# One layer with an RWKV-7 and a GLA mixer on one core: both heads of a pair multiplied by VectorE in one order, and chunk inverses from blocks of 16 joined by TensorE

## The chip, the cores and the metric

One core of one Trainium2 chip runs the whole kernel. The metric is device time in microseconds of one execution, the median of several runs. All arithmetic is fp32; wide matmuls are done as three products of rounded high and low halves.

## The reference, cut to what matters

An encoder layer works on two sequences of 512 and 256 tokens (768 together), model width 1024: a mixer, cross attention and a feed-forward net, each with norms. The mixer has eight RWKV-7 heads of width 64 and four GLA heads. An RWKV head keeps a 64x64 state S per direction (forward and backward) and goes from token to token:

```python
sa = einsum('bhij,bhj->bhi', S, -kk_t)
S = S * w_t[:, :, None, :] + sa[..., None] * (kk_t * a_t)[:, :, None, :] + v_t[..., None] * k_t[:, :, None, :]
y = einsum('bhij,bhj->bhi', S, r_t)
```

The kernel does this in chunks of 64 tokens, twelve in all. Within a chunk the products of decayed `kk` and `kk*a` make a strictly triangular 64x64 matrix N, and the chunk needs the inverse of I - N. That inverse is what half of this change is about.

## The kernel before, in words

Heads go in pairs p = 0 to 3, one head on partitions 0 to 63 and one on 64 to 127. For each pair, and each direction d:

- `prep` (L692) loads the projections, makes running sums of the decays, and with them two pair tiles: `bk_of` (L660) multiplies `kk*a` and `k` by the inverse decays, `ar_of` (L669) `kk` and `r` by the decays. Each of the eight products of a direction's two tiles covers one head (64 partitions, 12 chunks of 64): the first head's on VectorE (`dve`), the second's on GpSimd (`pool`). In the second head the two halves of a tile lie the other way round, so that a later matmul finds them in the order in which it wants them. `to_places` writes the tiles to DRAM (`bkd`, `ard`).
- `lower` (L678) makes N by 64x64 matmuls, copies it to `lsb`, and writes its 32x32 diagonal blocks to DRAM (`ld`).
- `inverses` (L731) reads the blocks of both directions so that each block lies in one partition (48 blocks a direction, 112 partitions with a gap), and inverts them there: 31 steps of a product and an addition on VectorE (L744, L746) on up to 256 elements a partition, in the tiles `snf`, `sqf`, `stmp`. Plain (`qd`) and transposed (`td`) results go to DRAM.
- `join` (L772) loads them back with channels on partitions (`tt`, `tdz`) and makes the missing 32x32 corner of each 64x64 inverse by two rounds of 32x32 matmuls, merge1 (L788) and merge2 (L800), 24 a direction; then the matrix goes to DRAM (`ttd`).
- `products` (L973) loads a group of four chunks of a pair and makes the matrices of a recurrence step; it transposes `bkg` for both heads (L1000).
- `stage(q)` (L1134) runs four `step`s (L1007) for up to three jobs: the recurrence, a chain that goes TensorE, ScalarE, TensorE, ScalarE, TensorE, VectorE and on to the next step.

Around them run other matmuls: the dense projections of the mixer (L247), the GLA heads (`gla_head`, L825), and sixteen `memory_block`s (L1104) for the cross attention's keys and values. The program is written pair by pair (`begin`, `invert`, `joined`), but the order on each engine is set by a scheduler from priorities: `high_priority(offset=...)` of 2000 for `begin` and `invert`, 6000 for `joined`, 4000 for the steps, 3000 for `products`. Each engine then works through its queue in that order. All transfers are issued by SyncE through `dma` (L41). In PSUM there are few banks: `psn` has one buffer, `psm` two.

## Time and profile before

| | |
|---|---|
| median of 3 runs | 1593.78 us (1593.54 to 1599.62) |
| profiled execution | 1596.87 us, span 1595.0 us |
| TensorE matmul busy | 1442.8 us, 90% of the span |
| VectorE, ScalarE, GpSimd busy | 1049.7, 718.9, 514.6 us |
| mean granted TensorE clock | 0.914 |
| DMA packets under 512 B | 89264 of 279565 |

The mixer's parts lie from about 120 to 840 us: `prep` of pairs 0 to 3 from about 142, 310, 467 and 542 us, the recurrence's steps from 444 to 826 us. After that come the output projection, the cross attention and the feed-forward net. A line of a view names the line of the kernel, the engine, the operation, and output<-inputs; x384 for 192 matmuls in the program means that the trace has two instructions for an fp32 matmul.

### The profile page before, as it was taken

To read this page: it belongs to the slowest core of one execution; us is meant where nothing else is said; L and a number is where in the kernel's file an instruction comes from. 1 tells how busy PE (TensorE), PEld (TensorE's weight loads), DVE (VectorE), ACT (ScalarE), POOL (GpSimd) and SP (SyncE) were. 2 spreads that over 40 slices of the span, in tenths; PEclk is the share of its full clock that TensorE was granted. 3 is DMA by queue.
4 is the path that set the end of the run, shared out by engine and by line. 5 is a ranking of instruction groups with operands and counts; after the bars stand their busy time and mean duration, and the time that the engine had idled before them with its cause. 6 is when DMAs were issued, how large, how long until landed. Compare 5 with 4: busy or idle time off the path is not lost. (4 is left out here: it accounts for less than half of the span.)

```text
span 1595.0 us, 28271 instructions
## 1 busy us (share of the span) xinstructions
PE 1442.8 (90%) x10614; PEld 1246.0 (78%) x10614; DVE 1049.7 (66%) x1605; ACT 718.9 (45%) x1417; POOL 514.6 (32%) x576
## 2 busy tenths in 40 slices
PE   7999689889887889899888999996999999999996
PEld 6887578777775777778767888786999999787785
DVE  5545885497577795764455434448876676878886
ACT  5754344443333332333344354434555556544442
POOL 6416643494317342211531354420000001231223
PEclk9999798989875988888979999997999999999998
DMA  6686555556468447754452333235555447564434
GB/s 168 181 302 188 167 137 131 145 146 192 111 205 229 127 149 176 205 134 135 126 166 99 119 95 105 73 111 160 172 169 176 158 145 284 171 204 132 143 100 142
DMA packets 279565, 250.35 MB, mean 157 GB/s; under 512 B 89264, under 2 KB 227059, under 8 KB 279428
## 3 DMA queue, kind: packets, MB, share of 16 engines
q1 hardware_dynamic: 279428, 248.54, 52.1%
q8 instruction: 84, 1.38, 0.4%
q14 instruction: 53, 0.43, 0.1%
HBM read 164.11 MB, written 82.58 MB: 155 GB/s over the span
## 5 line engine op out<-in xcount | busy, mean ns | idle before, releaser
L148 POOL TENSOR_TENSOR wlo<-wraw,whi 128x256 fp32r<-128x256 f32 x192 | 176.8, 934 | 331.0 <-ACT whi L147 231.1
L247 PE MATMUL pd<-hT_hi,whi 128*128 128x256 f32 (+1 forms) x512 | 182.0, 356 | 12.6 <-DVE gd L325 8.2
L247 PE MATMUL pd<-hT_hi,wlo 128*128 128x512 f32 (+1 forms) x512 | 180.1, 354 | 4.0 <-POOL wlo L148 4.0
L247 PE MATMUL pd<-hT_lo,whi 128*128 128x256 f32 (+1 forms) x512 | 178.6, 350 | 0.3 <-DVE hT_lo L206 0.3
L1511 POOL TENSOR_TENSOR wl<-w,wh 128x1024 fp32r<-128x1024 f32 x8 | 21.2, 2649 | 329.8 <-ACT wh L1510 329.8
L247 PEld LDWEIGHTS pd<-hT_hi,whi 128*128 128x128 f32 x512 | 100.4, 196 | 27.6 <-issue 5.5
L247 PEld LDWEIGHTS pd<-hT_hi,wlo 128*128 128x128 f32 x512 | 99.6, 195 | 18.6 <-POOL wlo L148 5.3
L147 ACT ACTIVATE whi<-wraw 128x256 fp32r<-128x256 f32 x192 | 77.3, 414 | 78.2 <-PE pd L1104 22.9
L247 PEld LDWEIGHTS pd<-hT_lo,whi 128*128 128x128 f32 x512 | 100.4, 196 | 13.0 <-DVE hT_lo L206 0.5
L148 DVE TENSOR_TENSOR ul<-ur,uh 128x768 fp32r<-128x768 f32 x56 | 77.4, 1388 | 30.7 <-ACT uh L147 17.7
L147 ACT ACTIVATE uh<-ur 128x768 fp32r<-128x768 f32 x56 | 47.4, 847 | 107.8 <-PE gz L1520 52.0
L1510 ACT ACTIVATE wh<-w 128x1024 fp32r<-128x1024 f32 x64 | 67.1, 1053 | 35.9 <-PE fz L1520 24.2
L1520 PE MATMUL gx<-wh,uh 128*128 128x512 f32 x192 | 75.0, 397 | 4.3 <-DVE acc L1713 4.3
L1511 DVE TENSOR_TENSOR wl<-w,wh 128x1024 fp32r<-128x1024 f32 x56 | 68.2, 1219 | 15.1 <-ACT wh L1510 14.5
L1520 PE MATMUL gx<-wl,uh 128*128 128x512 f32 x192 | 75.9, 395 | 0.0
L1520 PE MATMUL gx<-wh,ul 128*128 128x512 f32 x192 | 75.4, 395 | 0.0
L1520 PE MATMUL fz<-hh,wh 128*128 128x384 f32 x192 | 66.0, 344 | 1.9 <-ACT wh L1510 1.9
L1511 POOL TENSOR_TENSOR wl<-ws,wh 128x1024 fp32r<-128x1024 f32 x16 | 40.6, 2536 | 79.6 <-ACT wh L1510 79.6
L1520 PE MATMUL fz<-hh,wl 128*128 128x384 f32 x192 | 65.2, 344 | 0.8 <-DVE wl L1511 0.8
L1520 PE MATMUL fz<-hl,wh 128*128 128x384 f32 x192 | 65.8, 343 | 0.0
L1510 ACT ACTIVATE wh<-ws 128x1024 fp32r<-128x1024 f32 x48 | 50.5, 1052 | 26.8 <-PE fx L1520 22.3
L1104 PE MATMUL pd<-mem_hi,whi 128*128 128x256 f32 x256 | 59.3, 308 | 1.4 <-ACT mo L1116 1.4
(476 smaller groups left out, 4306.9 us busy)
## 6 DMA issues: line engine op xcount, KB each, us to landing
w<-in_w_ff_dram SPq DMA_DIRECT2D x64, 512.0 KB
ur<-ud SPq DMA_DIRECT2D x56, 384.0 KB
wraw<-in_w_in_dram SPq DMA_DIRECT2D x108, 128.0 KB
ud<-u SPq DMA_DIRECT2D x32, 384.0 KB
ud<-us SPq DMA_DIRECT2D x24, 384.0 KB
wraw<-in_wkv_x_dram SPq DMA_DIRECT2D x64, 128.0 KB
lora<-lo_t SPq DMA_DIRECT2D x20, 384.0 KB
bkg<-bkd SPq DMA_DIRECT2D x24, 256.0 KB
```

The source lines that it names most:

```text
L147: act.activation(out=hi, in_=src, func=AF.Copy)
L148: (lo_eng or pool).tensor_tensor(out=lo, in0=src, in1=hi, op=ALU.subtract)
L247: pe.matmul(out=out, lhsT=a, rhs=b, start=(i == 0), stop=(i == n - 1))
L1104: prev = order_after(pe.matmul(out=pd[:, c0:c0 + 256], lhsT=x, rhs=y[:, c0:c0 + 256], start=(k + i + c0 == 0), stop=(k + i + c0 == KD + 25 ...
L1510: act.activation(out=hi, in_=t[name], func=AF.Copy)
L1511: lo_eng.tensor_tensor(out=lo, in0=t[name], in1=hi, op=ALU.subtract)
L1520: pe.matmul(out=out, lhsT=a, rhs=b, start=first and i == 0, stop=last and i == n - 1, skip_group_check=True)
```

## The change

Two parts. **The products.** `bk_of` and `ar_of` now write both heads in one order, with one VectorE instruction over 128 partitions in place of one over 64 on VectorE and one over 64 on GpSimd. What read the second head in its old order is changed to match: `lower` and `products` take other indices, the load of `ard` for the second head becomes two transfers, and the transposes of the second head's `bkg` become four transposes of 64x64 and four matmuls by the identity, since the halves must change places.

**The inverses.** `lower` writes blocks of 16x16 (eight transfers in place of four a direction), `inverses` inverts pairs of those in 15 steps on up to 128 elements, and writes plain and transposed results into one tensor. `join` loads them into `inv` (plain and transposed, two 16x16 blocks on a diagonal of a 32x32 block that is zero elsewhere), and the off-diagonal 16x16 blocks of N from `lsb` into `offb`. Then for each direction: merge0 (48 matmuls of 32x32), an addition of the identity on VectorE, merge0t (24) and merge0m (48), and six copies on ScalarE; that gives what was loaded before. merge1 and merge2 follow as they were; merge2's copies go from VectorE to ScalarE. merge0 to merge0m use `psn` for the forward and `psm` for the backward direction, `tdz` now lies in `snf` and `stmp`, and the sums in `sqf` and `sxf`.

Since `snf`, `sqf` and `sxf` have become smaller, two of the planes for the output projection's weights and half of a gain row move to `inv` and `offb`; `t1` has two buffers in place of three.

```diff
     def bk_of(pinv, nka, kd):
         b_ = pair_tile()
-        dve.tensor_tensor(out=b_[0:64, :, 0, :], in0=v3(nka, 0, 64), in1=v3(pinv, 0, 64), op=ALU.mult)
-        pool.tensor_tensor(out=b_[64:128, :, 1, :], in0=v3(nka, 64), in1=v3(pinv, 64), op=ALU.mult)
-        dve.tensor_tensor(out=b_[0:64, :, 1, :], in0=v3(kd, 0, 64), in1=v3(pinv, 0, 64), op=ALU.mult)
-        pool.tensor_tensor(out=b_[64:128, :, 0, :], in0=v3(kd, 64), in1=v3(pinv, 64), op=ALU.mult)
+        dve.tensor_tensor(out=b_[:, :, 0, :], in0=v3(nka), in1=v3(pinv), op=ALU.mult)
+        dve.tensor_tensor(out=b_[:, :, 1, :], in0=v3(kd), in1=v3(pinv), op=ALU.mult)
...
-        for j in range(4):
-            dma(lds[st["p"]][d][:, j], lt[j * 32:(j + 1) * 32, :, (j % 2) * 32:(j % 2) * 32 + 32])
+        for j in range(8):
+            c = j % 4 * 16
+            dma(lds[st["p"]][d][j % 2, :, j // 2], lt[j * 16:(j + 1) * 16, :, c:c + 16])
...
-        for j in range(31):
-            nr, ni = j + 1, 31 - j
-            tm = stmp[:, 0:nr * ni].rearrange("p (a b) -> p a b", a=nr)
...
+        for j in range(15):
+            nr, ni = j + 1, 15 - j
+            tm = stmp[0:112, 0:2 * nr * ni].rearrange("p (e a b) -> p e a b", e=2, a=nr)
+            dve.tensor_tensor(out=tm, in0=sq[:, :, 0:nr, j:j + 1].broadcast_to([112, 2, nr, ni]),
+                              in1=sn[:, :, j:j + 1, j + 1:16].broadcast_to([112, 2, nr, ni]), op=ALU.mult)
+            dve.tensor_tensor(out=sq[:, :, 0:nr, j + 1:16], in0=sq[:, :, 0:nr, j + 1:16], in1=tm, op=ALU.add)
...
+            for j in range(8):
+                e, x = j % 2, j % 2 * 16
+                dma(invs[d][j * 16:j * 16 + 16].rearrange("p c q x -> p (c q) x")[:, :, x:x + 16],
+                    qd[d][e, :, j // 2].rearrange("s c q t -> s (c q) t"))
             for j in range(4):
-                rs = slice(j * 32, j * 32 + 32)
-                dma(tt[d][rs, :, (j % 2) * 32:(j % 2) * 32 + 32], qd[d][:, j])
-                if j % 2 == d:
-                    dma(tdz[d][rs], td[d][:, j])
+                r, c = 32 * j + 16 * d, j % 2 * 32 + 16 * (1 - d)
+                dma(offb[r:r + 16, d, :, 16 * (1 - d):16 * (1 - d) + 16], lts[d][r:r + 16, :, c:c + 16])
+        for d in range(2):
...
+            pm = bank("merge0")
+            for c in range(NCH):
+                for g in G:
+                    pe.matmul(out=pm[g, c, :], lhsT=offb[g, d, c, :], rhs=inv[g, c, 1, :], start=True, stop=True)
+            dve.tensor_tensor(out=fi, in0=pm, in1=bc(i32, NCH), op=ALU.add)
+            pm = bank("merge0t")
+            for c in range(NCH):
+                for g in G[d::2]:
+                    pe.matmul(out=pm[g, c, :], lhsT=inv[g, c, 0, :], rhs=fi[g, c, :], start=True, stop=True)
+            for g in G[d::2]:
+                act.activation(out=tdz[d][g], in_=pm[g], func=AF.Copy)
+            pm = bank("merge0m")
+            for c in range(NCH):
+                for g in G:
+                    pe.matmul(out=pm[g, c, :], lhsT=fi[g, c, :], rhs=inv[g, c, 0, :], start=True, stop=True)
+            for j, g in enumerate(G):
+                act.activation(out=tt[d][g, :, j % 2 * 32:j % 2 * 32 + 32], in_=pm[g], func=AF.Copy)
...
-            for h in (0, 64):
-                dve.tensor_copy(out=tt[d][h + o0:h + o0 + 32, :, o1:o1 + 32], in_=pn[h + o0:h + o0 + 32])
+            for h in (0, 64):
+                act.activation(out=tt[d][h + o0:h + o0 + 32, :, o1:o1 + 32], in_=pn[h + o0:h + o0 + 32], func=AF.Copy)
...
-        for h, hs in enumerate(HS):
-            dma(a_[hs, :, h:h + 2, :].rearrange("p u i x -> p u (i x)"), ard[p][hs, g])
+        dma(a_[HS[0], :, 0:2, :].rearrange("p u i x -> p u (i x)"), ard[p][HS[0], g])
+        for i in range(2):
+            dma(a_[HS[1], :, 2 - i, :], ard[p][HS[1], g, :, i * 64:i * 64 + 64])
...
-                pe.transpose(out=pt[:, u, :], in_=fl(b_[HS[h], u]), identity=ident[HS[h], HS[h]])
+                if h == 0:
+                    pe.transpose(out=pt[:, u, :], in_=fl(b_[HS[0], u]), identity=ident[HS[0], HS[0]])
+                else:
+                    pe.transpose(out=pt[HS[0], u, :], in_=b_[HS[1], u, 1, :], identity=ident[HS[1], HS[1]])
+                    pe.matmul(out=pt[HS[1], u, :], lhsT=b_[HS[1], u, 0, :], rhs=ident[HS[1], HS[1]], start=True, stop=True)
```

The scheduler's order moves with it. On TensorE, at pair 0's join, the order before had merge1 of the two directions (tiles `tdz`) with the last products of a GLA head (L913, L915) between them:

```order
L247 MATMUL pd<-hT_lo,whi 128x512
L788 MATMUL merge_2046<-tdz_1478,lsb 32x32 x24
L913 MATMUL go<-arena 128x64 x2
L915 MATMUL go<-arena 128x128
L913 MATMUL go<-arena 128x64 x2
```

Now the join comes while that GLA head has not begun its matmuls, among dense projections (L247). First the first rounds, with one lone merge0 ahead of them:

```order
L812 MATMUL merge_2028<-inv_1470,offb 32x32
L247 MATMUL pd<-hT_lo,whi 128x512
L247 MATMUL pd<-hT_hi,wlo 128x512
L247 MATMUL pd<-hT_hi,whi 128x512
L247 MATMUL pd<-hT_lo,whi 128x512
L247 MATMUL pd<-hT_hi,wlo 128x512
L247 MATMUL pd<-hT_hi,whi 128x512
L812 MATMUL merge_2028<-inv_1470,offb 32x32 x45
L812 MATMUL merge_2158<-inv_1474,offb 32x32 x37
L817 MATMUL merge0t<-sqf,inv_1470 32x32 x24
L812 MATMUL merge_2158<-inv_1474,offb 32x32 x11
```

Then, some twenty dense matmuls on, the rest in one piece:

```order
L247 MATMUL pd<-hT_hi,whi 128x256
L823 MATMUL merge0m<-inv_1470,sqf 32x32 x48
L817 MATMUL merge0t<-sxf,inv_1474 32x32 x24
L823 MATMUL merge0m<-inv_1474,sxf 32x32 x48
L833 MATMUL merge_2288<-snf,lsb 32x32 x24
L907 MATMUL gs<-arena 64x64 x12
```

The join moves ahead of the GLA head's matmuls, and the merges of the two directions alternate. On VectorE, in pair 0's inversion, the steps before stood among the evacuations of dense products (L322, L325):

```order
L744 TENSOR_TENSOR stmp<-sqf,snf 112x87
L322 SCALAR_TENSOR_TENSOR gd<-pd,cv,gd 128x511
L746 TENSOR_TENSOR sqf<-sqf,stmp 112x3x29
L325 SCALAR_TENSOR_TENSOR gd<-pd,cv,gd 128x511
L744 TENSOR_TENSOR stmp<-sqf,snf 112x112
L746 TENSOR_TENSOR sqf<-sqf,stmp 112x4x28
```

Now the same stretch of the inversion is:

```order
L761 TENSOR_TENSOR stmp<-sqf,snf 112x78
L763 TENSOR_TENSOR sqf<-sqf,stmp 112x2x3x13
L761 TENSOR_TENSOR stmp<-sqf,snf 112x96
L763 TENSOR_TENSOR sqf<-sqf,stmp 112x2x4x12
L761 TENSOR_TENSOR stmp<-sqf,snf 112x110
L763 TENSOR_TENSOR sqf<-sqf,stmp 112x2x5x11
```

Its first nine steps stand one behind the other with nothing between. On TensorE, at the recurrence's last steps, the order before had no memory blocks left, and output projections (`po`) between the steps (`rec`):

```order
L1049 MATMUL rec<-pl_5344 64x64 x4
L247 MATMUL po<-w_snf,mix_bk 128x512 x2
L247 MATMUL po<-w_sqf,mix_bk 128x512
L247 MATMUL po<-w_snf,mix_bk 128x512
L247 MATMUL po<-w_pl_9175,mix_bk 128x512 x3
L247 MATMUL po<-w_sqf,mix_bk 128x512
```

Now memory blocks (L1154 in the changed kernel) stand there:

```order
L1099 MATMUL rec<-pl_5841 64x64 x4
L1154 MATMUL pd<-mem_hi,whi 128x256
L1154 MATMUL pd<-mem_lo,whi 128x256 x2
L1154 MATMUL pd<-mem_hi,wlo 128x256 x2
L1154 MATMUL pd<-mem_hi,whi 128x256 x2
L1154 MATMUL pd<-mem_lo,whi 128x256 x2
```

The joins and the later steps have moved ahead of memory blocks: when the last step is reached, 672 of the 768 memory-block matmuls have been issued in the new order, and all 768 in the old one.

More of the change, by code (lines that the diff above doesn't have):

```diff
@@ L610 @@
         tts.append(t)
-        tdz.append(mp.tile([P, NCH, 32], F32, name=f"tdz{d}"))
+        t = mp.tile([P, NCH, 2, 32], F32, tag=f"inv{d}", name=f"inv{d}")
+        pool.memset(t, 0.0)
+        invs.append(t)
+    offb = mp.tile([P, 2, NCH, 32], F32, tag="offb", name="offb")
+    pool.memset(offb, 0.0)
+    i32 = mp.tile([P, 32], F32, name="i32")
+    for j in range(4):
+        rs = slice(32 * j, 32 * j + 32)
+        pool.tensor_copy(out=i32[rs], in_=ident[rs, rs])
     px = mp.tile([P, NCH, 66], F32, tag="px", name="px")
@@ L615 @@
     px_prev = (px[:, :, 0:64], px[:, :, 2:66])
[L616 to L618 removed]
+    snf, sqf, sxf = (mp.tile([P, 512], F32, tag=n, name=n) for n in ("snf", "sqf", "sxf"))
+    sn, sq, sx = (t[0:112].rearrange("p (e a b) -> p e a b", e=2, a=16) for t in (snf, sqf, sxf))
+    stmp = mp.tile([P, NCH * 32], F32, tag="stmp", name="stmp")
     pool.memset(sn, 0.0)
```

78 lines of the change are left out of this document (40 added, 38 removed).

## Prediction

> **What bounds the kernel now.** First the busy time of each engine by stretch (the columns are named in the head row; every field is a stretch's length, then busy time and instructions of an engine, then the TensorE clock that was granted). Two long stretches hold the mixer; eight short ones the places where VectorE is fullest, and the end of the recurrence.
>
> ```profile
> core 0: us, PE busy (x) PEld busy (x) DVE busy (x) ACT busy (x) POOL busy (x), PEclk, DMA share, GB/s
> 120.00:440.00 320.00, 276.36 (x1969) 232.64 (x1970) 223.35 (x278) 139.75 (x251) 169.74 (x165) 0.87 0.56 152
> 440.00:840.00 400.00, 348.01 (x4387) 291.33 (x4385) 263.90 (x598) 146.64 (x398) 133.71 (x150) 0.83 0.59 164
> ...
> 142.00:204.00 62.00, 47.49 (x328) 39.31 (x328) 50.97 (x36) 24.63 (x43) 46.41 (x41) 0.76 0.54 155
> 208.00:254.00 46.00, 40.14 (x263) 33.48 (x263) 44.08 (x88) 20.72 (x39) 16.31 (x19) 0.96 0.51 137
> 312.00:352.00 40.00, 34.51 (x227) 29.59 (x226) 38.94 (x25) 21.16 (x38) 38.07 (x25) 0.89 0.52 148
> 375.00:427.00 52.00, 45.14 (x235) 39.03 (x235) 41.07 (x79) 18.17 (x33) 15.63 (x13) 0.87 0.48 120
> 472.00:512.00 40.00, 26.47 (x322) 22.40 (x320) 32.99 (x43) 14.29 (x41) 31.87 (x27) 0.50 0.81 220
> 540.00:602.00 62.00, 52.52 (x733) 45.28 (x729) 58.66 (x116) 21.07 (x59) 30.07 (x24) 0.87 0.45 134
> 643.00:695.00 52.00, 45.50 (x612) 39.96 (x610) 47.50 (x129) 20.36 (x57) 10.86 (x15) 0.90 0.59 174
> 792.00:812.00 20.00, 10.02 (x88) 6.94 (x89) 14.36 (x29) 7.18 (x21) 14.22 (x21) 0.54 0.55 168
> ```
>
> TensorE is the engine that everything waits for in the end, and I count its loss as a stretch's length less busy time times granted clock, an estimate from above, since it takes a matmul at half the clock to last twice as long (the bursts quoted below last 0.95 and 1.49 us). From 120 to 440 us that is 320 - 276.36 x 0.87 = 80 us, from 440 to 840 us 400 - 348.01 x 0.83 = 111 us: 191 us in all. The four stretches in which `prep` runs (from 142, 312, 472 and 540) lose 25.9 + 9.3 + 26.8 + 16.3 = 78 us, with VectorE 82 to 97% busy; three in which `inverses` runs (208, 375, 643) lose 7.5 + 12.7 + 11.1 = 31 us at 79 to 96%; the recurrence's last steps (792) lose 14.6 us.
>
> Second, what the two engines do there: the groups by line, with mean ns, and the idle time before each at the end.
>
> ```profile
> L744 DVE TENSOR_TENSOR stmp<-sqf,snf 112x31 f32<-112x31 f32 (+15 forms) x124 | 53.1, 428 | 3.3
> L746 DVE TENSOR_TENSOR sqf<-sqf,stmp 112x31 f32<-112x31 f32 (+15 forms) x124 | 50.4, 406 | 3.0
> L685 PE MATMUL low<-bk 64*64 64x64 f32 x384 | 23.3, 267 | 16.6 <-DVE bk L672 16.6
> L674 POOL TENSOR_TENSOR bk<-r,px 64x768 f32<-64x768 f32 x8 | 19.2, 2396 | 0.0
> L672 DVE TENSOR_TENSOR bk<-kk,px 64x768 f32<-64x768 f32 x8 | 18.6, 2331 | 0.0
> L673 POOL TENSOR_TENSOR bk<-kk,px 64x768 f32<-64x768 f32 x8 | 18.5, 2306 | 0.0
> L663 DVE TENSOR_TENSOR bk<-wb,wa 64x768 f32<-64x768 f32 x8 | 18.1, 2267 | 0.0
> L675 DVE TENSOR_TENSOR bk<-r,px 64x768 f32<-64x768 f32 x8 | 17.2, 2145 | 0.0
> ```
>
> The two lines of the inversion take 103.5 us of VectorE. The products take more than 2.1 us apiece on either engine. Third, the order of time on VectorE shows why, and how long the inversion lasts by the clock: its first copy (L738) and its last (L752) for pairs 2 and 3, then two small steps of it.
>
> ```profile
> 159.23 0.95 DVE L665 TENSOR_TENSOR bk<-kds,wa 64x768 f32<-64x768 f32 x1
> 191.59 0.96 DVE L654 TENSOR_TENSOR wc<-wc,k 128x768 f32<-128x768 f32 x1
> 192.86 2.50 DVE L665 TENSOR_TENSOR bk<-wc,wa 64x768 f32<-64x768 f32 x1
> ...
> 526.84 0.69 DVE L738 COPY snf<-sxf 48x1024 f32<-48x1024 f32 x1 [5.13 <-DMA sxf<-ld]
> 608.71 1.04 DVE L752 COPY snf<-sqf 48x1024 f32<-48x1024 f32 x1
> 643.38 0.69 DVE L738 COPY snf<-sxf 48x1024 f32<-48x1024 f32 x1 [7.33 <-DMA sxf<-ld]
> 693.68 1.59 DVE L752 COPY snf<-sqf 48x1024 f32<-48x1024 f32 x1
> ...
> 208.97 0.19 DVE L744 TENSOR_TENSOR stmp<-sqf,snf 112x31 f32<-112x31 f32 x1
> 214.67 0.30 DVE L744 TENSOR_TENSOR stmp<-sqf,snf 112x135 f32<-112x135 f32 x1
> ```
>
> The same product lasts 0.95 us in one place and 2.50 us in the other, where GpSimd works on its own half beside it; a 128x768 product, twice the partitions, lasts 0.96 us. So the split between two engines gains nothing: each slows the other. And pair 2's inversion takes 83 us by the clock, pair 3's 52 us, because other VectorE work is queued between its steps. These two stand one behind the other: pair 3's cannot start before pair 2's `join` has left `sqf`, and the last two long stages of the recurrence need what they make. TensorE's order of time has the place where stage 2 waits for pair 2's matrix:
>
> ```profile
> 652.02 0.69 PE L1031 MATMUL rec<-rh,pl 64*64 64x64 f32 x8 [4.59 <-DMA pl<-ttd]
> ```
>
> The end of the kernel, from 880 us on, is dense TensorE work that the change does not touch; what the mixer gains or loses, the whole does.
>
> **The products, part by part.** Of 32 products of 64 rows on VectorE and 32 on GpSimd, 32 of 128 rows on VectorE are left. L663, L672 and L675 alone fall from 53.9 us to 24 x 0.96 = 23.0 us; L665 has runs at both 0.95 and 2.50 us, and I take 5 us for it. VectorE has some 36 us less to do, GpSimd some 74 us less (L673 and L674 with 37.7 us for 16 products, and L664 and L666 like them). GpSimd's other work, the low halves of weights, gets its turn earlier.
>
> **The inversion.** 62 steps on rows of up to 256 elements become 30 on up to 128. Elements per step: 2(j+1)(15-j), 1360 over the 15 values of j, so 91 in the mean. Between 31 elements at 0.19 us and 135 at 0.30 us, 91 take 0.25 us; 120 steps x 0.25 = 30 us against 103.5: 73 us less on VectorE, and about 1 us a pair of copies and fills that halve. With some 11 us a pair undisturbed (30 x 0.25 us, gaps and copies), the 83 and 52 us by the clock should fall to 15 to 25.
>
> **The joining.** `merge0`, `merge0t` and `merge0m` add 48 + 24 + 48 products of 32x32 a direction, 960 in all, each two instructions in the trace. Price, from a burst of the present merges and its successor, at full clock, and from a burst at half clock; then a transpose burst with its successor, and a burst of small matmuls with its own:
>
> ```profile
> 622.05 0.95 PE L788 MATMUL merge<-tdz,lsb 32*32 32x32 f32 x48
> 622.93 0.38 PE L1023 MATMUL rec<-pl 64*64 64x64 f32 x5
> ...
> 273.19 1.49 PE L788 MATMUL merge<-tdz,lsb 32*32 32x32 f32 x48
> ...
> 620.54 0.46 PE L1000 MATMUL bktp<-ident,bkg 64*128 64x64 f32 x4
> 620.92 0.38 PE L1104 MATMUL pd<-mem_hi,whi 128*128 128x256 f32 x1
> ...
> 627.49 0.45 PE L1038 MATMUL rec<-pl 128*64 128x64 f32 x8
> 627.87 0.32 PE L990 MATMUL scb<-pl,bkg 64*64 64x128 f32 x1
> ```
>
> 48 instructions hold TensorE 622.93 - 622.05 = 0.88 us at full clock, and up to 1.49 us at half. The 1920 new ones are 40 such bursts: 35 us, or 60 us. I take 38 us, since the order puts them into dense stretches. A rule to weigh here: the Trainium skill, "TensorE: Matmul & The Clock Gate", section "Wait — 56ns, not 53.3ns?", says that starts never follow closer than about 25 ns however small the matmul, and about 62 ns when instructions are decoded in ucode. By 25 ns the new ones would cost 48 us, by 62 ns 119 us; the trace has 0.88 us / 48 = 18 ns here, so neither floor holds for these. In `products` the second head's four transposes become four of half width and four matmuls (eight instructions): between nothing more and 627.87 - 627.49 = 0.38 us more, 24 times, 0 to 9 us; I take 6 us. The bursts of a join stand close together in the order, so a hand-over of a bank from TensorE to VectorE or ScalarE and back can stop TensorE: three more a direction. What such a piece takes is shown by the present ones, and by the copies that the change moves from VectorE to ScalarE:
>
> ```profile
> L792 ACT ACTIVATE sqf<-merge x16: 463/482/485, 265.6 to 721.5; 32x384 f32<-32x384 f32 x16
> L803 DVE COPY tt<-merge x16: 545/553/565, 283.9 to 730.7; 32x384 f32<-32x384 f32 x16
> ```
>
> One of 0.48 or 0.55 us is covered where the other direction's 48 instructions stand between (0.88 us), as they mostly do: I take 1 us a join, 4 us; bounds 0 (all covered) and 24 x 0.55 = 13 us. ScalarE gets 64 more pieces, 31 us, at 286 busy of 720 us; in its queue the evacuations behind them wait for the merges. VectorE loses 8.9 us and gets 8 sums of 0.55 us.
>
> **Transfers.** SyncE issues 26 more a pair (8 to leave `lsb`, 12 in `join`, 6 in `products`), 104 in all, and pieces shrink from 128 to 64 bytes. Before a join the last hop has 16 issues in place of 12:
>
> ```profile
> 256.76 2.18 SPq L41 DMA_DIRECT2D tt<-qd x2
> 259.03 0.42 SPq L41 DMA_DIRECT2D tdz<-td x1
> ```
>
> At 0.42 to 1.1 us each, four more are 2 to 4 us later; the eight of `offb` need only `lsb` and go ahead of the inversion. That sits in a chain that has become 30 to 60 us shorter, so I set no time for it, and 4 x 4 = 16 us as the far bound, if TensorE stands at each first `merge0` for it.
>
> **The sum.** Added TensorE time: 38 + 6 + 4 = 48 us. Against it stands what comes back of the loss. Of the 78 us in the `prep` stretches I take 65%: the products that filled both engines become half on one and nothing on the other, and TensorE's waits for them (16.6 us at L685) and the slow-clock stretches behind them go; what stays are scans and transfers. Of the 31 us beside the inversions, half; of the last 14.6 us, half, because the order leaves memory-block matmuls to lay between the last steps. 51 + 16 + 7 = 74 us. The net is 26 us: the profiled execution, 1596.87 us with a span of 1595.0, would become 1571 us; it lay 3.1 us above the median of 1593.78, so 1568 us.
>
> **Rivals.** *Joins that stop TensorE (slower).* TensorE takes its queue in order, and in the new order one lone `merge0` stands before dense matmuls. If the blocks land late, everything behind waits, and the clock drops: the 4.59 us wait at 652 is such a place. Eight such stops (one a direction) with as much lost again to the half clock are 8 x 9 = 73 us; the forecast's 26 turn into 47 lost: 1641. It decides from 26/8 = 3.3 us of loss a direction on; half the full price, 36 us, gives 1604. For it: a first join that stands among dense matmuls in the new order. Against: the new last hop is little longer. Chance 0.2, with 1604 as its likely size.
>
> *The loss is not VectorE's (no change).* 111 us of loss lie after 440 us, where the chain of the recurrence goes from engine to engine and DMA is 59% busy. If only 40% of the 78, 30% of the 31 and 20% of the 14.6 come back, 43 us, the 48 added eat it: 1599 by the sum, with a merge price of 35 us 1596. Chance 0.15, together with its mild form, that 128-row products are still slowed by GpSimd's work on weights (as L665 at 192.86 beside it), in which the change does not do what it says for the products.
>
> *The chain was the bound (much faster).* If the 83 and 52 us of the two inversions were what held stages 2 and 3, and TensorE then finds filler everywhere, another 30 us of the 111 come back: 1538. For it: VectorE is 95% busy from 540 to 602. Against: TensorE was 85% busy there too. Chance 0.2.
>
> **How the numbers follow.** The forecast has 0.45, the rivals 0.2, 0.15 and 0.2. Faster or slower means by more than 8 us, 0.5%, about what a measurement of this kernel can tell. The forecast's own range is 1550 to 1590 (merges at 60 us take 22 us back; at 35 us, with 85% of the `prep` loss, 18 us more come): 0.43 of its 0.45 is faster, and with the last rival that makes 0.63. Same gets 0.15, slower 0.22, the 0.2 of the first rival and a little of the second. The range for 8 in 10 reaches into both outer rivals: 1533 to 1606.
>
> **What would show it.** Right: products of 128x768 near 0.96 us; inversion steps near 0.25 us and 15 to 25 us by the clock; the clock in the `prep` stretches (0.76 and 0.50 in the two worst) near full; merge0 groups at some 18 ns an instruction. Wrong: TensorE idle before `merge0` for a transfer, products still over 2 us, or a granted clock from 440 us on that stays near 0.83.

## The result, and the profile after

The changed kernel takes 1690.26 us (median of 4 runs, 1688.49 to 1696.39) against 1595.54 us for the kernel before (4 runs, 1593.54 to 1599.62): a ratio of 1.062, with a 95% interval of 1.059 to 1.065. That is 95 us slower, where 26 us faster was forecast. The profiled execution took 1688.49 us, with a span of 1686.8 us and a mean granted clock of 0.897.

The prediction's terms on VectorE came out in the direction that was forecast, if not in full. The groups by line of the changed kernel, one row each for the two lines of the inversion, for three of the products (all are on 128 rows now) and for TensorE's `low`:

```profile
L763 DVE TENSOR_TENSOR sqf<-sqf,stmp 112x30 f32<-112x30 f32 (+7 forms) x60 | 20.1, 335 | 1.7
L761 DVE TENSOR_TENSOR stmp<-sqf,snf 112x30 f32<-112x30 f32 (+7 forms) x60 | 19.6, 327 | 1.6
L673 DVE TENSOR_TENSOR bk<-wb,wa 128x768 f32<-128x768 f32 x8 | 11.4, 1423 | 0.0
L680 DVE TENSOR_TENSOR bk<-kk,px 128x768 f32<-128x768 f32 x8 | 11.4, 1420 | 0.0
L681 DVE TENSOR_TENSOR bk<-r,px 128x768 f32<-128x768 f32 x8 | 8.6, 1081 | 0.0
L691 PE MATMUL low<-bk 64*64 64x64 f32 x384 | 19.0, 247 | 7.7 <-DVE bk L680 6.3 <-ACT lsb L693 1.4
```

The inversion's 103.5 us are 39.7 us, the products take 1.1 to 1.4 us in place of 2.3, and TensorE's wait at `low` fell from 16.6 to 7.7 us. An inversion takes little time by the clock as well, 14 us for pair 3 where it took 52, from its first copy to its last on VectorE:

```profile
653.33 0.42 DVE L754 COPY snf<-sxf 48x512 f32<-48x512 f32 x1 [4.66 <-DMA sxf<-ld]
...
667.01 0.61 DVE L769 COPY snf<-sqf 48x512 f32<-48x512 f32 x1
```

Still the kernel is slower, so the time must be sought on TensorE. Busy time by stretch, after (columns as in the prediction):

```profile
142.00:204.00 62.00, 48.97 (x324) 40.75 (x322) 39.68 (x58) 20.89 (x42) 23.46 (x31) 0.88 0.67 185
208.00:254.00 46.00, 41.62 (x797) 35.68 (x797) 6.79 (x12) 18.67 (x36) 6.61 (x10) 0.76 0.38 71
120.00:440.00 320.00, 279.56 (x2817) 237.24 (x2816) 153.81 (x202) 140.57 (x257) 120.21 (x148) 0.83 0.54 140
440.00:840.00 400.00, 356.84 (x5103) 295.13 (x5102) 194.27 (x472) 142.11 (x371) 70.59 (x80) 0.78 0.50 132
840.00:920.00 80.00, 55.55 (x467) 47.61 (x466) 27.27 (x60) 32.13 (x74) 37.79 (x59) 0.85 0.49 145
```

and the last of these stretches before:

```profile
840.00:920.00 80.00, 74.77 (x369) 61.65 (x370) 39.65 (x68) 31.59 (x83) 22.20 (x38) 0.98 0.34 109
```

VectorE is much freer (48% busy where it was 70% from 120 to 440 us), yet TensorE's loss has grown. By the prediction's measure (length less busy time times clock) the three long stretches lose 88 + 122 + 33 = 243 us where before lost 80 + 111 + 7 = 198 us. The same measure over the whole span, in stretches of 20 us, splits each span into idle time, time lost to the clock, and TensorE work at full clock: 152 + 106 + 1337 us before, 160 + 139 + 1388 us after. So 51 us of the 92 are more TensorE work, 33 us a lower clock and 8 us idle time. The forecast had 48 us of work, but 74 us less loss. One of the prediction's own signs of being wrong is here: the granted clock from 440 to 840 us did not rise from 0.83, it fell to 0.78.

Two things in the trace stand out. First, the GLA heads and the recurrence begin much later. The rows of the tiles `gs` (first matmul of a GLA head) and `rec` (first and last rows of a step), with first and last start at the end of each: before

```profile
L862 PE MATMUL gs<-arena x192: 218/267/366, 143.1 to 372.5; 64*64 64x64 f32 x192
L1018 PE MATMUL rec<-pl x384: 218/222/369, 443.8 to 814.7; 128*64 128x64 f32 x160, 64*64 64x64 f32 x32
L1049 PE MATMUL rec<-pl x384: 222/222/369, 450.7 to 826.1; 128*64 128x64 f32 x192
```

and after:

```profile
L907 PE MATMUL gs<-arena x192: 218/267/366, 239.7 to 448.7; 64*64 64x64 f32 x192
L1068 PE MATMUL rec<-pl x384: 218/270/369, 504.2 to 871.6; 128*64 128x64 f32 x160, 64*64 64x64 f32 x32
L1099 PE MATMUL rec<-pl x384: 222/222/369, 518.3 to 878.6; 128*64 128x64 f32 x192
```

The first GLA head starts 97 us later, behind the first join, and the recurrence 60 us later. At its end TensorE then stands for the operand of the output projection, a wait that was 1.29 us before:

```profile
912.62 1.19 PE L247 MATMUL po<-w_snf,mix_bk 128*128 128x512 f32 x2 [23.00 <-POOL mix_px L148]
```

Second, the transposes of `bkg`. Groups of TensorE by line, before (48 groups of four transposes) and after (head 0's transposes, then head 1's transposes and matmuls by the identity):

```profile
L1000 PE MATMUL bktp<-ident,bkg 64*128 64x64 f32 x192 | 25.1, 259 | 3.1 <-DVE pl L994 1.8 <-DVE pl L996 1.3
```

```profile
L1050 PE MATMUL bktp<-ident,bkg 64*64 64x64 f32 x192 | 35.5, 272 | 0.0
L1049 PE MATMUL bktp<-ident,bkg 64*64 64x64 f32 x96 | 25.1, 262 | 1.0 <-DVE pl L1042 0.8 <-DVE stmp L761 0.2
L1047 PE MATMUL bktp<-ident,bkg 64*128 64x64 f32 x96 | 13.8, 269 | 2.1 <-DVE pl L1040 2.0
```

Durations of matmuls overlap, so I count what a group holds TensorE as the time from its start to the next instruction's start, without TensorE's idle time in it, summed over the order of time: 21.9 us before, 11.6 + 18.1 + 25.2 = 54.9 us after. One group of head 1 shows where it goes:

```profile
618.77 0.24 PE L1049 MATMUL bktp<-ident,bkg 64*64 64x64 f32 x1
618.94 0.33 PE L1050 MATMUL bktp<-ident,bkg 64*64 64x64 f32 x2
619.20 0.24 PE L1049 MATMUL bktp<-ident,bkg 64*64 64x64 f32 x1
619.37 0.33 PE L1050 MATMUL bktp<-ident,bkg 64*64 64x64 f32 x2
```

A transpose and a matmul (two instructions) take 0.43 us together, and four such pairs 1.7 us, where four transposes took 0.38 us in the prediction's row.

The joins' new rounds themselves hold TensorE 11.2 + 7.3 + 9.4 = 27.9 us, and 11.7 us of idle time lie before them: 39.6 us, against 38 forecast. Their form is not the forecast's: long bursts at 12 ns an instruction, stops for which the trace names no releaser, and stretches at half the clock behind them. The first join in the order of time:

```profile
222.33 2.08 PE L812 MATMUL merge<-inv,offb 32*32 32x32 f32 x163
224.23 0.19 PE L817 MATMUL merge0t<-sqf,inv 32*32 32x32 f32 x1
...
227.20 0.69 PE L817 MATMUL merge0t<-sqf,inv 32*32 32x32 f32 x18 [2.36 <-issue]
...
229.32 0.41 PE L247 MATMUL pd<-hT_hi,whi 128*128 128x256 f32 x1
229.53 0.41 PE L247 MATMUL pd<-hT_lo,whi 128*128 128x256 f32 x1
...
250.52 0.53 PE L247 MATMUL pd<-hT_hi,whi 128*128 128x512 f32 x1
250.89 0.39 PE L247 MATMUL pd<-hT_lo,whi 128*128 128x512 f32 x1
251.12 0.39 PE L247 MATMUL pd<-hT_hi,wlo 128*128 128x512 f32 x1
```

At 229 us a 128x256 matmul follows the last after 0.21 us, where at full clock one of 128x512 follows after 0.23 (250.89 to 251.12 us), and no dense matmul runs at that pace again before 250.9 us. So there were three candidates: the joins' small instructions (A, later A1), the turn between transposes and matmuls (B), and the order with its late tail (C).

### The profile page after: what moved, and what is told of

It reads as the page before. It is cut to its first block, busy times and chain, and to the rows that moved or that the text cites. A ratio compares the mean times of both kernels' runs of the same rounds, so it can differ in the third digit from the quotient of the medians.

```text
span 1686.8 us, 32554 instructions
## 1 busy us (share of the span) xinstructions
PE 1526.8 (91%) x12726; PEld 1315.4 (78%) x12726; DVE 941.0 (56%) x1473; ACT 751.7 (45%) x1481; POOL 442.3 (26%) x551
## 4 chain that ended last, share of the span: by engine, by line
PE 46%; DVE 7%; issue 6%; DMA 2%; POOL 1%; ACT 1%; SPq 0%; DVEq 0%; POOLq 0%; ACTq 0%
PE fx L1570 7%; PE gx L1570 7%; PE fz L1570 5%; PE gz L1570 5%; PE pd L1154 4%; PE pd L247 4%; PE po L247 3%; PE xo L247 1%; DVE ws L1510 1%; DVE wl L1561 1%; PE rec L1068 1%; PE xs L247 1%; PE bktp L1050 1%; POOL rs L1288 1%; PE rec L1099 1%
## 5 line engine op out<-in xcount | busy, mean ns | idle before, releaser
L148 POOL TENSOR_TENSOR wlo<-wraw,whi 128x256 fp32r<-128x256 f32 x192 | 170.1, 898 | 495.0 <-ACT whi L147 381.6
L247 PE MATMUL pd<-hT_hi,whi 128*128 128x512 f32 (+1 forms) x512 | 189.0, 369 | 6.1 <-ACT gd L476 3.7
L247 PE MATMUL pd<-hT_hi,wlo 128*128 128x256 f32 (+1 forms) x512 | 184.1, 362 | 5.1 <-POOL wlo L148 5.1
L247 PE MATMUL pd<-hT_lo,whi 128*128 128x512 f32 (+1 forms) x512 | 184.3, 361 | 0.3 <-DVE hT_lo L206 0.3
L247 PEld LDWEIGHTS pd<-hT_hi,whi 128*128 128x128 f32 x512 | 104.1, 203 | 22.1 <-ACT gd L476 4.1
L247 PEld LDWEIGHTS pd<-hT_hi,wlo 128*128 128x128 f32 x512 | 104.0, 203 | 20.7 <-POOL wlo L148 7.2
L247 PEld LDWEIGHTS pd<-hT_lo,whi 128*128 128x128 f32 x512 | 104.4, 204 | 14.2 <-issue 0.7
L1154 PE MATMUL pd<-mem_hi,whi 128*128 128x256 f32 x256 | 64.3, 324 | 1.1 <-ACT whi L147 1.1
```

The lines of the kernel that those rows point to most:

```text
L148: (lo_eng or pool).tensor_tensor(out=lo, in0=src, in1=hi, op=ALU.subtract)
L247: pe.matmul(out=out, lhsT=a, rhs=b, start=(i == 0), stop=(i == n - 1))
L1154: prev = order_after(pe.matmul(out=pd[:, c0:c0 + 256], lhsT=x, rhs=y[:, c0:c0 + 256], start=(k + i + c0 == 0), stop=(k + i + c0 == KD + 25 ...
```

## The experiments

Ratios are against the kernel before, measured beside each run, with 95% intervals. 0.01 is 16 us. Where I split a run's time into idle time, clock and work, it is as above, of its profiled execution.

**The two halves of the change.** `p1_products` is the kernel before with the new `bk_of`, `ar_of`, `products` and the changed index in `lower`; `p2_inverses` is the rest of the change.

> The kernel before with the products part of the change alone (inverses in blocks of 32 and the old join). Theory A (the joins cost it: their small rounds are followed by stretches at half the granted clock): without the new joins nothing of the loss is here, and the products give back what the prep stretches gained in the changed kernel, some 15 to 20 us, less 6 for the transposes: about 1584. Theory B (the second head's transposes, taken in turn with matmuls, hold TensorE 54.9 us in place of 21.9 us, 33 us more): 1595 + 33 - 17 = about 1611. Theory C (the order's tail: memory blocks left between the last steps, then 23.0 us of TensorE idle before the output projection for a load of the mixer's result): shows only if this kernel's order has that tail too; 1595 + 23 = 1618 without B, and TensorE idle there is seen in the waits.

> The kernel before with the inverses part of the change alone (products split between VectorE and GpSimd as before, single transposes). Theory A: the joins' new rounds hold TensorE 28 us, wait 12 us, and their stretches lose 77 us of clock and idle time where the old joins lost 25 us: 1595 + 40 + 40 less some 10 us for the shorter inversion = about 1665. Theory B: the price of the joins is only the 38 to 40 us that they hold TensorE, and the shorter inversion gives 16 to 20 back: about 1617, with the granted clock in the join stretches near 0.9. Theory C: a wait of some 20 us before the output projection if memory blocks are left to the end.

p1: 1.009 (1.006 to 1.012), 1602 us. p2: 1.053 (1.049 to 1.056), 1672 us. The halves add up to the whole (0.009 + 0.053 against 0.062). A's number was met for p2 (1665 us expected), but by luck: most of its reason fell later.

**The turn of transpose and matmul.** `p3_grouped`:

```diff
-                    pe.matmul(out=pt[HS[1], u, :], lhsT=b_[HS[1], u, 0, :], rhs=ident[HS[1], HS[1]], start=True, stop=True)
+            if h:
+                for u in range(4):
+                    pe.matmul(out=pt[HS[1], u, :], lhsT=b_[HS[1], u, 0, :], rhs=ident[HS[1], HS[1]], start=True, stop=True)
```

> The changed kernel with the second head's eight instructions of a group in another order: four transposes, then four matmuls by the identity, in place of one and one in turn. Same work, same instructions. Theory A: within 5 us of the changed kernel, 1685 to 1690. Theory B: if the turn between transpose and matmul is what costs (0.43 us a pair at full clock where four transposes take 0.46 us in all), it falls by some 25 us: about 1665, and the matmuls by the identity take 0.05 to 0.06 us an instruction in place of 0.13. Theory C: unchanged, 1690.

`p4_swap` takes `products` as it was and loads head 1's halves into their old places:

```diff
-        dma(b_, bkd[p][:, g])
+        dma(b_[HS[0]], bkd[p][HS[0], g])
         for i in range(2):
+            dma(b_[HS[1], :, 1 - i, :], bkd[p][HS[1], g, :, i])
```

> The changed kernel with the second head's halves of bkg put in their old places by the load from DRAM (three transfers in place of one, 48 more in all), so that its matmuls and its four transposes are those of the kernel before. Theory A: 1690 less 6 = about 1684. Theory B: the whole 33 us go: about 1657, and bktp holds TensorE some 22 us again. Theory C: the tail stays unless the order changes: 1690 or, with B, 1657.

p3: 1.043 (1.040 to 1.047). p4: 1.043 (1.040 to 1.047). Both take 0.019 off the changed kernel, some 29 us. In p3 the same twelve instructions stand together:

```profile
601.71 0.41 PE L1049 MATMUL bktp<-ident,bkg 64*64 64x64 f32 x4
602.04 0.68 PE L1052 MATMUL bktp<-ident,bkg 64*64 64x64 f32 x8
```

Four transposes hold TensorE 0.33 us here, and over all groups `bktp` holds it 35.1 us in place of 54.9. The only edit against the changed kernel is the order inside a group, so the cost of the turn is shown. How it reaches the whole is less clear: p3 gains 29 us where the hold shrinks by 20, p4 the same where it shrinks by 33. By the split, p3 has 29 us less clock loss, 10 us less work and 5 us more idle time than the changed kernel. `p6_products_grouped` does the same edit in p1:

> The products part alone (p1), with the second head's four transposes of a group ahead of its four matmuls by the identity. Theory B from the first four runs: products and joins add up, the turn of transpose and matmul costs some 30 us in either place. p1 stood 14 us above the kernel before, so 14 - 28 = 14 us below it: about 1574, ratio 0.991. If the turn costs only where the joins are too (theory A takes it in), it stays at p1's 1.009, about 1602.

p6: 0.996 (0.994 to 0.998), 0.013 or 21 us below p1. It is the one version that beats both kernels, by 6 us.

**What the products give.** `p5_products_swap` is p1 with p4's load, so that TensorE's instructions are those of before.

> The products part alone, with the second head's halves put in their old places by the load (as in p4), so that TensorE's work is that of the kernel before: what is left is the move of the 64 products of 64 rows to 32 of 128 rows on VectorE. By the prediction's own step (51 us back of the 78 us lost in the prep stretches): 1592 - 51 = 1541, ratio 0.968. By what the prep stretches of the changed kernel show (some 15 us back) : about 1577, ratio 0.990. By p6 (0.996, with the grouped instructions): 6 us better than that, 0.992, or the same where the grouped ones hide.

p5: 1.000 (0.999 to 1.002). The move of the products to VectorE alone is worth nothing. Its stretches:

```profile
120.00:440.00 320.00, 283.31 (x2096) 239.07 (x2096) 207.64 (x289) 143.10 (x255) 125.54 (x150) 0.87 0.58 156
440.00:840.00 400.00, 329.83 (x4222) 277.69 (x4221) 240.01 (x587) 142.98 (x394) 98.22 (x134) 0.83 0.59 159
```

and its wait at `low`, 16.6 us before:

```profile
L681 PE MATMUL low<-bk 64*64 64x64 f32 x384 | 21.2, 264 | 5.5 <-DVE bk L670 4.8 <-ACT lsb L683 0.7
```

From 120 to 440 us the loss fell from 80 to 74 us, from 440 to 840 us it rose from 111 to 126. As I read it, TensorE does earlier what it is given earlier, and the recurrence, whose chain is no shorter, has less left to lay over it; no run tests that reading alone. That p6, with more TensorE work, stands 7 us below p5 is not explained; the two have different orders, and I take it as the size of what the order alone can do.

**The joins' small instructions.** `j1_wide` replaces each new round's 32x32 matmuls by 12 of 128 rows against the identity, and so leaves the merging itself out:

```diff
-                for g in G:
-                    pe.matmul(out=pm[g, c, :], lhsT=offb[g, d, c, :], rhs=inv[g, c, 1, :], start=True, stop=True)
+                pe.matmul(out=pm[:, c, :], lhsT=ident, rhs=inv[:, c, 1, :], start=True, stop=True)
```

> The changed kernel with each new round of a join as 12 matmuls of 128 rows by 32 against the identity, in place of 48 (merge0, merge0m) or 24 (merge0t) of 32 by 32: 72 instructions a direction in place of 240, with the same chain of hand-overs between TensorE, VectorE and ScalarE. It leaves out the merging itself: the rounds pass their blocks on unmerged, the output is not the reference's. Theory A1 (the number of small instructions costs: TensorE runs them faster than they come, stands for 1.5 to 2.4 us without a releaser, and the clock is at half for some 20 us behind): the stops go and most of the half clock, some 40 us less, about 1645. Theory A2 (the chain of hand-overs and the place in the order cost): within 10 us of the changed kernel, 1680 to 1690.

j1: 1.099 (1.095 to 1.102), 58 us slower than the changed kernel. I had mispriced the wide fp32 matmul:

```profile
L811 PE MATMUL merge<-inv,ident 128*128 128x32 f32 x192 | 28.7, 314 | 5.8 <-DMA inv<-qd 5.8
L820 PE MATMUL merge0m<-sxf,ident 128*128 128x32 f32 x96 | 18.9, 371 | 0.0
```

The stops without a releaser are gone, but the rounds hold TensorE 97.7 us in place of 27.9. 70 more, less the 6 us of idle time that went (11.7 to 5.8), is 64 us, and 58 were measured: here TensorE time in a join was paid nearly in full, and taking the stops away gave at most their own length. The clock did not come back with them. While the new rounds hold TensorE, the mean granted clock is 0.65 in j1 and 0.78 in the changed kernel, and by the split j1 loses 41 us more to the clock. In j1's first join the clock is at half from 222.8 to 260.3 us without a stop of TensorE over 0.3 us. So the half clock needs neither 32x32 matmuls nor these stops, and j1 does not price what the small ones lose by it. `d1_burst` is the other way round, the burst without the rest, in the kernel before:

```diff
+        for d in range(2):
+            pm = (psn, psm)[d]("burst")[:, 0:NCH * 32].rearrange("p (c x) -> p c x", x=32)
+            for c in range(30):
+                c = c % NCH
+                for j in range(4):
+                    g = slice(32 * j, 32 * j + 32)
+                    blk = tt[d][g, c, j % 2 * 32:j % 2 * 32 + 32]
+                    pe.matmul(out=pm[g, c, :], lhsT=blk, rhs=blk, start=True, stop=True)
         fts = []
```

> The kernel before with 120 more 32x32 matmuls a direction at each join (the same number as the change's new rounds), which read the blocks that the join has loaded and whose results nobody reads: the small instructions alone, without a hand-over, a new transfer or another inversion. Theory A1: 8 bursts of 240 instructions at 12 to 15 ns hold TensorE 23 to 29 us, each pair of bursts has a stop of about 2 us without a releaser and 20 us at half clock behind it (10 us lost): 1588 + 26 + 8 + 40 = about 1660. Theory A2: only what they hold TensorE, 1588 + 26 = about 1614, with the granted clock in the joins near that of before.

`d2_quarter` has 28 of these matmuls a direction, `d6_four` has 4.

> The kernel before with bursts as in d1, but 28 matmuls a direction in place of 120 (56 instructions a direction, 112 a join, where d1 had 480). If the price goes by the number (81 us for 1920 instructions): 19 us, 1611, ratio 1.012. Theory A1 (TensorE stands once it has run through the instructions at hand, of which d1 shows 128 between two stops): no stop, little half clock, 448 instructions at 14 ns = 6 us: 1598, ratio 1.004.

> The kernel before with d1's insertion at 4 matmuls a direction in place of 120: 64 instructions in all, under 1 us of TensorE time, but with another order from the scheduler, since it places them too. Theory A1 (the small instructions themselves, by stops and clock): same as before, 1594, ratio within 0.995 to 1.005. Theory A3 (any insertion there moves the order, and waits for operands come up elsewhere, as the 27 us more of idle time in d2 show): some 20 to 40 us slower, ratio 1.012 to 1.025.

d1: 1.051 (1.047 to 1.055). d2: 1.030 (1.028 to 1.033). d6: 1.037 (1.033 to 1.042). d1 alone would have confirmed A1: nearly the whole price of p2, from the bursts alone. The doses overthrow that, and neither theory had d2 or d6 so dear. 64 instructions, expected to take under 1 us (they hold TensorE 4 us), cost 57 us, and the 1856 more of d1 only 22 us, less than their hold (26.4 us for all) and their stops without a releaser (21 us in all). The price hangs mostly on the insertion, not on what is inserted. It does not follow the dose either: d2, with seven times d6's instructions, is 11 us faster, so the order alone moves such a figure by some 10 us.

**The buffer.** What d6 has in common with the change is `psm`. Its two PSUM buffers are handed out in the program's order, and in the program `joined(0)` (L859 of the changed kernel) stands ahead of `gla_head(0)` (L980). As long as a join took only `psn`, the GLA heads could overtake it. Now a join takes a turn in `psm`, and `gs`, `gds` and `gsum`, whose turns come after, wait for it. The order of TensorE says so. In the kernel before, the first GLA head stands at row 610 (143.1 us in the trace), the first merge1 nearly four hundred rows later (261.0 us):

```
L463 MATMUL gvt<-ident,gd 128x128 x4
L862 MATMUL gs<-arena 64x64 x18
L463 MATMUL gvt<-ident,gd 128x128 x2
```

in the changed kernel its first row is 914, behind the join's new rounds:

```
L823 MATMUL merge0m<-inv_1474,sxf 32x32 x48
L833 MATMUL merge_2288<-snf,lsb 32x32 x24
L907 MATMUL gs<-arena 64x64 x12
```

`k1_four_psn` is d6 with `psn` for both directions, `k2_psn` the changed kernel with the same edit:

```diff
-                return (psn, psm)[d](name)[:, 0:NCH * 32].rearrange("p (c x) -> p c x", x=32)
+                return psn(name)[:, 0:NCH * 32].rearrange("p (c x) -> p c x", x=32)
```

> d6_four (64 tiny instructions inserted in the joins of the kernel before) with both directions' results in psn, none in psm. Theory A4 (the new work takes a turn in psm's two buffers, and whatever has its turn behind it, GLA heads above all, must come after the join): the GLA heads stand ahead of the joins again, the order is nearly that of before, and the 57 us go: 1594, ratio 0.995 to 1.008. Theory A3 (any insertion moves the order and costs): stays near d6's ratio of 1.037.

> The changed kernel with merge0, merge0t and merge0m of both directions in psn, none in psm. The directions then take turns in psn's single buffer, so a join has a longer chain of hand-overs. Theory A4: of the changed kernel's 98 us, the turn of transposes (28 us) and the time that the rounds hold TensorE (28 us) stay, the rest goes: about 1645, ratio 1.03. If the joins cost by their small instructions and half clock (A1): no better than the changed kernel, 1.06.

k1: 1.016 (1.012 to 1.019), 35 us below d6. k2: 1.031 (1.027 to 1.036), 49 us below the changed kernel, although its joins now have one buffer for both directions. The two pairs are not equally clean. From d6 to k1, with no long burst in either, 33 us of the profiled difference of 36 are idle time of TensorE, 14 of them ahead of the output projection. From the change to k2 it is 33 us of idle time and 24 us of clock against 5 us more work, and there the edit does more than move the turn: the rounds come apart. Where the changed kernel runs 146 to 255 small instructions up to a stop of 1.4 to 2.4 us without a releaser, no piece in k2 has more than 96 and no such stop is over 1.1 us, and the granted clock during the new rounds is 0.97 in place of 0.78. So A1 may hold a part of k2's 49 us; the 35 us are the cleaner price of the turn. First GLA head and first step, in d6:

```profile
L869 PE MATMUL gs<-arena x192: 218/218/365, 246.5 to 447.9; 64*64 64x64 f32 x192
L1025 PE MATMUL rec<-pl x384: 216/267/369, 523.6 to 845.1; 128*64 128x64 f32 x160, 64*64 64x64 f32 x32
```

in k1:

```profile
L869 PE MATMUL gs<-arena x192: 218/218/366, 144.0 to 380.1; 64*64 64x64 f32 x192
L1025 PE MATMUL rec<-pl x384: 216/222/369, 445.6 to 832.0; 128*64 128x64 f32 x160, 64*64 64x64 f32 x32
```

and in k2:

```profile
L907 PE MATMUL gs<-arena x192: 218/218/313, 146.4 to 375.5; 64*64 64x64 f32 x192
L1068 PE MATMUL rec<-pl x384: 218/270/369, 443.0 to 854.6; 128*64 128x64 f32 x160, 64*64 64x64 f32 x32
```

All kernels here fall into these two kinds. In those whose join takes `psm` (the change, p2, p3, p4, j1, j2, d1, d2, d6, r1) `gs` begins between 237 and 258 us and the recurrence between 502 and 528; in all others between 143 and 147, and between 436 and 458. k1's remaining 25 us for 64 instructions stay open: the burst waits for `tt` ahead of merge1 in TensorE's queue (seven waits, 5.2 us in all, the longest 1.7), and the order is not quite that of before.

**The tail.** `j2_mixdve` is the changed kernel with ScalarE and VectorE splitting the operand of the output projection:

```diff
-            load_split(mixd[k], *mix[k], lo_eng=pool)
+            load_split(mixd[k], *mix[k], lo_eng=dve)
```

> The changed kernel with the halves of the mixer's result, the operand of the output projection, made by ScalarE (high) and VectorE (low) in place of GpSimd for both. Theory C: TensorE's 23.0 us of idle time ahead of the output projection is the 36 us chain of loads and GpSimd work behind the last memory weights, of which GpSimd's 21 casts and 21 low halves are 0.40 and 0.73 us each, 24 us; with two engines in place of one the wait falls to 8 to 12 us: about 1677. If the loads themselves set the end (21 transfers from 875.5 to 908.6 us), the wait stays near 20 and the time at 1690.

j2: 1.048 (1.044 to 1.052), 22 us faster (its profiled execution, the slowest of four, 10 us), and the wait is 10.41 us in place of 23.00:

```profile
901.92 0.79 PE L247 MATMUL po<-w_snf,mix_bk 128*128 128x512 f32 x1 [10.41 <-ACT w_snf L147]
```

In k2 it is 1.8 us without that edit, so in the changed kernel the buffer brought the wait too. It is not bound to the late order as such: n1 below, whose GLA heads begin at 147 us, waits 26.5 us there, and d2, with the late order, 3.4 us. `b1_best` puts the edit into p5, where the wait was short:

> p5 (products on VectorE in one order, halves put in place by the load, old inverses and joins) with the operand of the output projection split by ScalarE and VectorE (j2). If the chain of loads before the output projection is covered by the last steps there (2.3 us of wait in p6): the same as p5, 0.992. If it sets the start of the output projection, up to 10 us less: 0.986.

b1: 1.007 (1.004 to 1.009), no gain, 10 us worse than p5. `r1_repaired` is p3 with j2's edit, `k3_repaired_psn` the same with `psn` alone.

> The whole change with the two shown costs undone: transposes of the second head ahead of its matmuls (p3), and the operand of the output projection split by ScalarE and VectorE (j2). If they add up: ratio 1.062 less 0.018 (p3) less 0.014 (j2) = 1.030, about 1641; what then stands over the kernel before, some 47 us, is the joins. If the tail's wait is only passed on to the next one, p3's 1.043.

> r1 (transposes ahead of matmuls, operand of the output projection split by ScalarE and VectorE) with the joins in psn alone. Theory A4: k2 less 28 us for the transposes, the tail being gone with the order: 1610 to 1620, ratio 1.01 to 1.017; what is left is the rounds' own time on TensorE, less what the products and the shorter inversion give. A1: as r1, 1.036.

r1: 1.036 (1.033 to 1.039); j2's gain came through only by half. k3: 1.019 (1.016 to 1.023), 27 us below r1. With these three costs undone the change is still 30 us slower than before. That the rounds hold TensorE about as long is chance in part: by the split k3 has 49 us more TensorE work than before and 32 us less loss (10 us idle, 22 us clock). In k3, too, no piece of the rounds has over 96 instructions, and what lies between r1 and k3 is mostly clock: 33 us less lost to it and 4 us less idle time, against 9 us more work.

**The shorter inversion alone.** `n1_norounds` is p4 with these lines in place of the new rounds and of the loads of `offb`, so that it leaves out joining the blocks of 16; `n2_norounds_mix` has j2's edit besides.

```diff
+        for d in range(2):
+            tdz[d] = invs[d][:, :, 1, :]
+            for j, g in enumerate(G):
+                act.activation(out=tt[d][g, :, j % 2 * 32:j % 2 * 32 + 32], in_=invs[d][g, :, 0, :], func=AF.Copy)
```

> The changed kernel with the second head's halves put in place by the load (p4) and without the three new rounds of the join: merge0, merge0t, merge0m and the transfers to offb are left out, and the blocks of 16 go on as if the 32x32 blocks held nothing else, so the output is not the reference's. Inversion and transfers are those of the change. If the shorter inversion and the products give what the prediction took for them (16 + 51 us): 1592 - 67 = 1525, ratio 0.958. Theory A with the products' gain as measured (p6): the price of the rounds was p4's 1.043 less this; the inversion's own gain small, 0 to 16 us: 1570 to 1585, ratio 0.986 to 0.996. If the rounds' place is only a small part of the loss (the 16-blocks' transfers or the order cost): 1620 or more, ratio over 1.017.

> n1 (the change with halves put in place by the load and without the joins' new rounds, whose merging is left out, so that the output is not the reference's) with the operand of the output projection split by ScalarE and VectorE (j2), which takes most of n1's 26.5 us wait ahead of the output projection. If the shorter inversion is worth what the prediction took (16 us), the time falls below p5's: 1595 - 16 = about 1579, ratio 0.99. If nothing is left of it: about n1 less 15, 1600, ratio 1.004.

n1: 1.014 (1.012 to 1.017). n2: 1.007 (1.004 to 1.010). So the inversion in 16s gains nothing even where its joining costs nothing, net of its smaller transfers and its copies on ScalarE, which both kernels keep and no run takes apart. It does shorten the chain it stands in: the last step of the recurrence starts at 787 us in n2, 39 us earlier than before.

```profile
L1075 PE MATMUL rec<-pl x384: 222/266/370, 464.7 to 787.1; 128*64 128x64 f32 x192
```

But the output projection starts at 831 us there (808 before): TensorE had memory blocks left, did them without the steps to lay them between, and then waited 10.5 us for the operand.

## Why the prediction was wrong, point by point

- *"I count its loss ... TensorE is the engine that everything waits for in the end."* Right for what is held: of the 70 us that j1 added to TensorE's hold, the kernel took 58 longer. But the count left out that an edit can move the loss itself, as d6 does with 4 us of hold.
- *VectorE's terms.* Right in direction, a third to a half too low: inversion 39.7 us (30 forecast, 0.33 us a step for 0.25), products 40.8 us in all (28 forecast, 66.2 before; 1.1 to 1.4 us each for 0.96). By the clock an inversion takes 14 to 21 us (15 to 25 forecast).
- *"The 1920 new ones ... I take 38 us."* Right as a sum, by luck: the term was TensorE's time alone, which is 27.9 us, and 11.7 us of idle time make up the rest. The prediction's "neither floor holds" was a misreading: it set a floor for each matmul against the trace's instructions, and the program has half as many matmuls as the trace has instructions. 163 instructions in 1.90 us are 23 ns a matmul of the program. The Trainium skill, "TensorE: Matmul & The Clock Gate", section "Wait — 56ns, not 53.3ns?", has about 25 ns as the floor of a matmul. The trace is near it, a little below.
- *"between nothing more and ... 0 to 9 us; I take 6 us"* for the second head's transposes. **Failed, by five times**: they hold TensorE 33 us more, and cost 21 (p1 to p6) to 29 us (change to p3). The row I priced from was a burst of eight instructions of one kind; the new code takes turns between two kinds, and the turn is what costs.
- *"hand-over of a bank ... 1 us a join, 4 us."* **Failed by leaving the larger cost of the same buffer out.** I asked who evacuates a bank and not who has the next turn in it. The order I quoted showed the join ahead of the GLA head's matmuls, and I took it for a move of the join. It was the GLA head that had moved back, and with it the start of the recurrence, 60 us. Putting the rounds into `psn` is worth 27 (r1 to k3), 35 (d6 to k1) or 49 us (change to k2, the 23 us wait ahead of the output projection among them); of the three pairs only d6 and k1 are free of long bursts.
- *"51 + 16 + 7 = 74 us"* coming back. **Failed whole**: p5 shows 0 of the 51, n2 none of the 16. The waits named did shrink (16.6 to 5.5 us at `low` in p5), but the same work lay there as cover for what follows, and the loss came up again after 440 us. (In k3 the loss is 32 us less than before, beside 49 us more work; whether that is some of the 74, no run shows.) I had a rival for this (the loss is not VectorE's), at 0.15.
- *The slower rival* had the sign and not the place: waits of merge0 for its blocks from DRAM are 2.9 us in all. Its full price was 1641 us, and no rival of mine reached 1690.

The costs don't quite add: 29 us (turn) + 49 us (buffer) + 30 us (what k3 leaves) are 108 of the 98 us at this ratio, since part of each lies in the others' stretches, and the 49 may hold some of the bursts' clock as well.

## What to carry to other kernels

Before pricing a new use of a shared buffer, list whose turn comes after it in the program: a buffer handed out in program order is a barrier for everything behind it, however short the new work. When an insertion costs far more than its own time, insert next to nothing in the same place; if the price stays, look at what the insertion binds, not at what it does. Time given back on an engine off the bound was worth nothing here; before counting on it, show what the bound does earlier and what then covers its later waits.

## What the runs showed of the hardware

Transposes and matmuls in turn: 0.43 us a pair at full clock, where in p3 four transposes together hold TensorE 0.33 us at full clock and four matmuls by the identity 0.65 us in the mean (15.6 us for 192 instructions).

Long bursts of small matmuls come to a stop. In d1's first burst, of one kind, TensorE stops after 191 instructions and then after each 128, while the trace shows nothing that it waits for:

```profile
244.56 1.80 PE L788 MATMUL burst<-tt 32*32 32x32 f32 x191
249.05 1.93 PE L788 MATMUL burst<-tt 32*32 32x32 f32 x128 [2.69 <-issue]
253.05 1.93 PE L788 MATMUL burst<-tt 32*32 32x32 f32 x128 [2.07 <-issue]
256.51 0.48 PE L788 MATMUL burst<-tt 32*32 32x32 f32 x19 [1.53 <-issue]
```

128 instructions last 1.9 us and the next come after 4.00 and 3.46 us, so this burst goes on at 27 to 31 ns an instruction. d1's other bursts stop first after 158 to 249 instructions, and where they go on long enough, again after 128. What the stop waits for, the trace does not name.

The clock fell with no long stop. The changed kernel's first join, cut where the granted clock changes (columns as above):

```profile
226.91:233.74 6.83, 6.54 (x83) 6.06 (x87) 0.56 (x1) 2.81 (x6) 1.49 (x3) 0.50 0.29 79
233.74:237.16 3.42, 2.01 (x189) 1.91 (x180) 0.00 (x0) 2.44 (x6) 0.71 (x1) 1.00 0.33 82
237.16:250.81 13.65, 13.16 (x215) 11.65 (x215) 2.22 (x4) 8.21 (x15) 1.55 (x3) 0.50 0.13 41
```

It fell to half at 226.9 us, in a stop of 2.36 us behind a long burst. It came back to full at 233.7 us, after 6.5 us of busy TensorE, dense matmuls from 228.3 us on. It fell again at 237.2 us, in a second stop of 1.90 us behind a burst, and stayed at half to 250.8 us, through a stretch in which small and dense matmuls lie mixed and TensorE is 96% busy. In j1's first join, where matmuls of 128x32 take the place of the small ones, it fell at 222.8 us with no stop at all, and was still at half through this stretch, in which the profile has TensorE busy from end to end:

```profile
227.00:260.27 33.27, 33.27 (x266) 32.01 (x265) 2.78 (x5) 11.09 (x21) 1.57 (x3) 0.50 0.04 10
```

So being busy by the profile did not by itself keep the clock up here. What would have, no run here shows. The Trainium skill, "TensorE: Matmul & The Clock Gate", section "Part 1: The HAM clock gate", has the clock fall after an idle window of about 3.4 us and rise after as long a busy one. The rise at 233.7 us agrees with that. The falls came with less idle time, and j1's clock did not rise in 33 us of what the profile calls busy; there the measurement decides.
